# 17 pairs of column blocks as 2x2 block products in seven multiplications, in a hybrid trunk layer

## The chip, the cores and the metric

The kernel runs on one core of one Trainium2 chip. The metric is device time in microseconds (us) of one execution. The engines are named as the profile names them: PE is TensorE (matmuls; PEld its weight loads), DVE is VectorE, ACT is ScalarE, POOL is GpSimd, SP is SyncE, which here issues DMAs.

## The reference, cut to what matters

One layer over 512 prompt tokens and 64 sample tokens (T = 576), D = 1024, all fp32:

```python
h = _rmsnorm(x, norm_pre_w)
proj = h @ w_in                       # 1024 x 13344
glu_v, glu_g, conv_gate, z, xbc, dt_raw, q, xa_gate, gates = split(proj)

u = glu_v * sigmoid(glu_g)            # A: conv branch
c = causal_dwconv(u, width 31)
c = silu(layernorm(c)) * silu(conv_gate)
out_a = c @ conv_out_w
...                                   # B: state-space branch from z, xbc, dt_raw
out_b = y @ ssd_out_w
p = softmax(q @ mem_k / 16)           # C: 4 heads, 256 memory tokens
out_c = ((p @ mem_v) * silu(xa_gate)) @ xa_out_w

g = sigmoid(gates + gate_b)           # three gates, 1024 wide each
m = g[0] * out_a + g[1] * out_b + g[2] * out_c
x_new = x + _rmsnorm(m @ w_out, norm_post_w)
```

For the prompt, mem_k and mem_v are themselves a product, rmsnorm(mem) @ xa_kv_w; for the sample they come from a cache. The names used below for columns of w_in: `glu j` is the pair of column blocks gg (glu_g) and gv (glu_v); `cg` is conv_gate; `xg` is xa_gate; `g0`, `g1`, `g2` are the three gates. A block is 128 columns, so xg, g0, g1 and g2 have eight blocks each and q eight, two for each head.

## The kernel before, in words

The normed input is kept transposed, channels on partitions, as two tiles `hT[0]` and `hT[1]`: the rounded fp32r value and the remainder ("hi" and "lo"). Each weight block is 1024 x 128 and is one job of the list `order`. `prep_to` loads a job into `raw` by a DMA on SP's queue (512 KB), copies it to `whi` on ACT (L183) and lets DVE subtract to get `wlo` (L184); `W(name)` prepares up to LA = 2 jobs past the one asked for. Each of raw, whi and wlo has three buffers. `mac` (L204) multiplies in three passes (wh·rh, wh·rl, wl·rh), for eight k-tiles and two halves of 288 tokens: 48 matmuls of 288 columns for a block of w_in. `proj` returns the two PSUM banks of it.

The order of instructions on each engine is made by a scheduler at build time that estimates times; some are held in program order. The stages on PE, by the trace: the start and the state-space groups with glu 0 to 2 and out_b (to 503 us), glu 3 and 4 with the eight g1 blocks (to 573.7), four attention heads with their two xg blocks each and glu 5 to 7 (to 808), the g2 blocks in turn with the merge products oc (to 908), cg and g0 (to 1010), the merges oa (to 1062), and w_out.

Beside these, DVE works off a list of convolution steps in the background: for each of eight channel blocks 30 taps over 606 columns (L769, `c<-u,dww,c`), pushed in pairs by `push_conv` so that two blocks alternate, and taken n at a time by `bgrun(n)`.

A head of the attention computes k and q blocks, v, the scores (L886 to L888), a softmax (maxima L871 on DVE, exps L875 and scalings L880 on ACT), then xg's two blocks, then transposes P (L937, L944), splits it (L940, L941, L946), multiplies with v ("PV", again L886 to L888, and L956) and writes `oc` times the gate (L953, L959). The memory tokens' transposes (`memT`, L321 and L322) stand between the g1 blocks.

The core of the block product before the change:

```python
for i, (wh, wl, rh, rl) in enumerate(pairs, k0):
    for w, r, a in ((wh, rh, 0), (wh, rl, 1), (wl, rh, 2)):
        for o, (s, w_) in outs:
            m = nc.tensor.matmul(o, lhsT=w, rhs=r[:, s:s + w_], ...)
```

Of the kernel before, what the change touches and what calls it, by code (L numbers as in the profile page):

```python
# [15 lines left out]
T = 576  # L16
# [12 lines left out]
def hybrid_trunk_kernel(  # L29
# [134 lines left out]
    nprep = [0]  # L164

    def prep_to(n):
        while nprep[0] <= min(n, len(order) - 1):
# [14 lines left out]
            else:  # L182
                a = nc.scalar.activation(hi[:, :n_], raw[:, :n_], AF.Copy)  # L183
                b = nc.vector.tensor_tensor(lo[:, :n_], raw[:, :n_], hi[:, :n_].bitcast(F32), ALU.subtract)  # L184
# [534 lines left out]
    def glu(j, pool, tag, bufs, rate=4):  # L719
# [4 lines left out]
        bgrun(rate)  # L724
        pv = proj(f"gv{j}", HB)
        u = sx.tile([128, 640], F32, tag="xs", name="u", bufs=7)
        nc.gpsimd.memset(u[:, 0:30], 0.0)
        nc.gpsimd.tensor_copy(u[:, 542:572], sta.rearrange("p (r j) -> p r j", r=30)[:, :, j])
        nc.vector.scalar_tensor_tensor(v2(u[:, 30:542]), v2(t[:, 0:512]), 1.0, pv[:, :, 0:256], ALU.add, ALU.mult)
        nc.vector.scalar_tensor_tensor(u[:, 572:636], t[:, 512:T], 1.0, pv[:, 1, 256:320], ALU.add, ALU.mult)  # L730
        nc.gpsimd.tensor_scalar(utail[:, j, 0:30], u[:, 512:542], 0.5, None, ALU.mult)
        nc.gpsimd.tensor_scalar(utail[:, j, 30:60], u[:, 606:636], 0.5, None, ALU.mult)
        upad[j] = u
        bgrun(rate)
# [74 lines left out]

    for j in range(8):  # L810
        t = gate_t(f"g1_{j}", 1, j, sx, "xs", 7)
        nc.vector.scalar_tensor_tensor(ob[:, j], t, 1.0, ob[:, j], ALU.add, ALU.mult)
        nc.sync.dma_start(out=msc[j], in_=ob[:, j])
        bgrun(6)
        tr_act(mt_, j, memT, V_MEM, NMEM)
    stob.close()
    ocp = stx.enter_context(tc.tile_pool(name="ocp", bufs=1, side="right", reuse_waits="tile"))
# [72 lines left out]
    for h in range(4):  # L890
# [38 lines left out]
        for i in range(2):  # L929
            sgs.append(silu2(proj(f"xg{2 * h + i}"), sx, "xs", 7))  # L930
# [53 lines left out]
    ochl = [split(oc[:, j]) for j in range(8)]  # L984
    ocact = ([a for a, _ in ochl], [b for _, b in ochl])
# [39 lines left out]
    for j in range(8):  # L1025
        merge(j, 2, f"g2_{j}", f"oc{j}", ocact)
# [7 lines left out]
    stx.close()  # L1034
    stx = ExitStack()


    hlB = stx.enter_context(tc.tile_pool(name="hlB", bufs=8, side="right", reuse_waits="tile"))
    hl[0] = hlB
    chl, g0t = [], []  # L1040
    for j in range(8):
# [11 lines left out]
        g0t.append(gate_t(f"g0_{j}", 0, j, hlA, "lo", 8))  # L1053
# [138 lines left out]
```

## Time and profile before

| what | value |
|---|---|
| median of 3 runs | 1122.61 us (1122.55 to 1123.11) |
| the profiled execution | 1122.15 us, its span 1120.4 us, granted PE clock 0.999 |
| PE busy, instructions | 1109.5 us, 8285 |
| DVE busy, instructions | 829.1 us, 1268 |
| ACT busy, instructions | 481.9 us, 844 |
| POOL busy, instructions | 56.8 us, 146 |
| data moved | 120.74 MB, mean 108 GB/s |

The span runs from the first to the last instruction; the execution adds 1.75 us around it. An engine's busy time is a sum over the whole span, so its share says little about one stage: the windows show the stages apart. In a row of a group, `out<-in` gives the names of the tiles, then shapes, the count, the busy time and the mean of one in ns, and behind the bar the idle time of the engine just before these instructions with what ended it.

### The profile page before, as it was taken

The page shows a single profiled execution, that of the slowest core. Times are in us where ns is not written, and L with a number is a line of the kernel's source. Part 1 is how long each engine was busy: PE and PEld are TensorE (multiplying, and loading weights), DVE is VectorE, ACT ScalarE, POOL GpSimd, SP SyncE. Part 2 cuts the span into 40 slices and gives each one's busy share as a digit, 9 for nine tenths or more (in the row PEclk, how much of TensorE's full clock was granted, in tenths as well). Part 3 has the DMA queues.
Part 4 walks back from the last instruction along what each step waited for, and adds up shares of the span by engine and source line. Part 5 has one row for each costly group of instructions (what it writes and reads, how often), then busy time and mean ns, then how long its engine had stood idle before and what let it go on. Part 6 is the DMA issues. An engine that isn't in the chain of part 4 may idle for free.

```text
span 1120.4 us, 20083 instructions
## 1 busy us (share of the span) xinstructions
PE 1109.5 (99%) x8285; PEld 1070.9 (96%) x8285; DVE 829.1 (74%) x1268; ACT 481.9 (43%) x844; POOL 56.8 (5%) x146
## 2 busy tenths in 40 slices
PE   8999999999999999999999999999999999999997
PEld 8999999999999999999999999999999999999974
DVE  5778897578868885756899996998588868714533
ACT  5564664456436442543224453434421245522331
POOL 0100110011002100100000000000000000000000
PEclk9999999999999999999999999999999999999999
DMA  7354423442353232242445343434353234233502
GB/s 208 95 162 122 143 82 94 129 117 81 97 144 107 83 81 78 75 124 76 135 139 142 85 131 95 123 85 116 84 160 93 76 84 106 76 94 104 178 20 85
DMA packets 183233, 120.74 MB, mean 108 GB/s; under 512 B 12422, under 2 KB 173230, under 8 KB 183142
## 3 DMA queue, kind: packets, MB, share of 16 engines
q1 hardware_dynamic: 183142, 119.46, 37.4%
q8 instruction: 65, 1.06, 0.4%
q14 instruction: 26, 0.21, 0.1%
HBM read 110.13 MB, written 9.31 MB: 107 GB/s over the span
## 4 chain that ended last, share of the span: by engine, by line
PE 97%; DMA 1%; ACT 1%; SPq 0%; DVE 0%; issue 0%; DVEq 0%; ACTq 0%
PE mm L204 78%; PE ps L204 4%; PE ps L887 2%; PE ps L886 2%; PE ps L888 2%; PE ps L561 2%; PE ps L587 2%; PE ps L565 1%; DMA ob<-in_x_prompt_dram 1%; PE ps L526 1%; PE ps L1130 1%; PE ps L518 1%; PE mm L346 0%; DMA out_dram<-ho 0%; PE ps L483 0%; PE ps L937 0%
## 5 line engine op out<-in xcount | busy, mean ns | idle before, releaser
L204 PE MATMUL mm<-hT,whi 128*128 128x288 f32 (+2 forms) x3328 | 588.3, 297 | 0.8 <-DVE hT L280 0.3
L204 PEld LDWEIGHTS mm<-hT,whi 128*128 128x128 f32 x3328 | 495.1, 189 | 3.6 <-issue 1.3
L204 PE MATMUL mm<-hT,wlo 128*128 128x288 f32 (+2 forms) x1664 | 363.9, 297 | 0.0
L183 ACT ACTIVATE whi<-raw 128x1024 fp32r<-128x1024 f32 x152 | 160.9, 1059 | 401.0 <-PE mm L204 323.9
L204 PEld LDWEIGHTS mm<-hT,wlo 128*128 128x128 f32 x1664 | 273.6, 189 | 1.1 <-issue 0.7
L184 DVE TENSOR_TENSOR wlo<-raw,whi 128x1024 fp32r<-128x1024 f32 x152 | 185.8, 1222 | 116.0 <-ACT whi L183 115.7
L769 DVE SCALAR_TENSOR_TENSOR c<-u,dww,c 128x606 f32<-128x606 f32 x240 | 191.5, 844 | 0.0
L204 PE MATMUL mm<-hi,whi 128*128 128x288 f32 x512 | 111.4, 298 | 0.0
L204 PE MATMUL mm<-lo,whi 128*128 128x288 f32 x512 | 110.9, 296 | 0.0
L204 PE MATMUL mm<-hi,wlo 128*128 128x288 f32 x512 | 110.4, 296 | 0.0
L204 PEld LDWEIGHTS mm<-hi,whi 128*128 128x128 f32 x512 | 82.2, 189 | 0.9 <-issue 0.9
L204 PEld LDWEIGHTS mm<-hi,wlo 128*128 128x128 f32 x512 | 82.5, 188 | 0.2 <-issue 0.2
L204 PEld LDWEIGHTS mm<-lo,whi 128*128 128x128 f32 x512 | 82.5, 188 | 0.0
L454 DVE SCALAR_TENSOR_TENSOR acc<-xp,scw,acc 128x579 f32<-128x579 f32 x72 | 58.4, 815 | 3.1 <-ACT acc L450 1.9
L658 DVE TENSOR_TENSOR ob<-ob,mm 128x576 f32<-128x576 f32 x24 | 18.0, 750 | 16.3 <-PE mm L204 16.2
L547 ACT ACTIVATE M<-R,tok 128x128 f32<-128x128 f32 (+1 forms) x80 | 24.8, 379 | 12.3 <-PE ps L587 12.3
L446 POOL COPY tails<-xp 128x3 f32<-128x3 f32 x24 | 18.0, 751 | 193.2 <-ACT xp L444 187.9
L887 PE MATMUL ps<-lo,hi 128*128 128x512 f32 x64 | 25.3, 397 | 0.0
L888 PE MATMUL ps<-hi,lo 128*128 128x512 f32 x64 | 25.1, 395 | 0.0
L886 PE MATMUL ps<-hi 128*128 128x512 f32 x64 | 24.9, 397 | 0.0
L565 PEld LDWEIGHTS ps<-bc,h 128*128 128x128 f32 x128 | 16.5, 191 | 8.8 <-issue 6.6
L204 PE MATMUL ps<-whi,memT 128*128 128x256 f32 x128 | 23.5, 282 | 0.0
(292 smaller groups left out, 1287.8 us busy)
## 6 DMA issues: line engine op xcount, KB each, us to landing
raw<-in_w_in_dram SPq DMA_DIRECT2D x104, 512.0 KB
R<-scr SPq DMA_DIRECT2D x16, 512.0 KB
raw<-in_ssd_out_w_dram SPq DMA_DIRECT2D x16, 512.0 KB
raw<-in_xa_kv_w_dram SPq DMA_DIRECT2D x16, 512.0 KB
raw<-in_xa_out_w_dram SPq DMA_DIRECT2D x8, 512.0 KB
raw<-in_conv_out_w_dram SPq DMA_DIRECT2D x8, 512.0 KB
wraw<-in_w_out_dram SPq DMA_DIRECT2D x8, 512.0 KB
E<-scr SPq DMA_DIRECT2D x24, 128.0 KB
```

The costliest lines, as they stand in the source:

```text
L183: a = nc.scalar.activation(hi[:, :n_], raw[:, :n_], AF.Copy)
L184: b = nc.vector.tensor_tensor(lo[:, :n_], raw[:, :n_], hi[:, :n_].bitcast(F32), ALU.subtract)
L204: m = nc.tensor.matmul(o, lhsT=w, rhs=r[:, s:s + w_], start=(i == 0 and a == 0), stop=(i == n - 1 and a == 2),)
L454: nc.vector.scalar_tensor_tensor(acc, xp[:, r:r + 579], w4[:, r, jt:jt + 1], acc, ALU.mult, ALU.add)
L547: nc.scalar.activation(M[:, 4 + e, :], R[:nl, 4 + e, :], AF.Relu, scale=-1.0, bias=tok[:nl, 0, c, a + 4:a + 5])
L561: nc.tensor.matmul(pS, lhsT=bt[:nl], rhs=xw[:nl], start=True, stop=True)
L565: nc.tensor.matmul(po[:, nl * j:nl * j + nl], lhsT=h[:, 128 * j:128 * j + 128], rhs=gC[g][:, cs], start=True, stop=True,)
L587: nc.tensor.matmul(pd[o:o + 64, nl * (e // 2):nl * (e // 2) + nl], lhsT=xd[:nl, 64 * e:64 * e + 64], rhs=M[:, e, :], start=True, stop=True,)
L769: nc.vector.scalar_tensor_tensor(c, upad[j][:, r:r + NC], w31[:, r, j:j + 1], c, ALU.mult, ALU.add)
L886: nc.tensor.matmul(out, lhsT=wh, rhs=rh, start=(i == 0), stop=False)
L887: nc.tensor.matmul(out, lhsT=wh, rhs=rl, start=False, stop=False)
L888: nc.tensor.matmul(out, lhsT=wl, rhs=rh, start=False, stop=(i == n - 1))
```

## The change

All in `hybrid_trunk_kernel`:

- 17 pairs of blocks, in the order glu 3, g1 (four pairs), glu 4 to 7, xg (four), g2 (four), are computed in one stretch right behind out_b(3). For a pair the two blocks' columns, the two halves of the 1024 channels, and the two halves of the tokens make a 2x2 block product, which is done by seven products P1 to P7 (Strassen in Winograd's form) of 4 k-tiles x 3 passes = 12 matmuls of 288 columns.
- The combinations of hT (T1 to T4, hi and lo) are built once at the stretch's start by DVE and ACT. The weight-side sums (s1 to s4) are made by DVE for each pair, with their hi by ACT and lo by DVE. The blocks used unchanged (W11, W12, W22) get their hi by an ACT copy, and their lo by an ACT copy with factor -1 and a POOL-issued DMA that adds raw to it.
- The results are put together from three kinds of PSUM banks (X, Y, Z, two of each) with copies on ACT and adds on DVE. xg (with its silu) and g2 (its tanh) go to DRAM (`spill`) and are loaded back in the heads and merges.
- The 56 weight jobs behind the stretch get their lo by the same ACT copy and accumulating DMA in place of DVE's subtract.
- q0 and q1 come ahead of k0; memT's transposes stand behind q0 and q1 and no longer between g1 blocks. Convolution blocks from the third on are pushed singly; one background step is taken at every second slot of the stretch; the convolution's result is copied back over its input. The heads lose their xg and glu products. Some pools move.

```diff
-    for j in range(3, 5):
-        glu_jobs(j)
-    for j in range(8):
-        wjob(f"g1_{j}", w_in, C_G + 1024 + 128 * j)
+    hold = len(order)
     for h in range(4):
+        if h == 0:
+            for i in range(2):
+                wjob(f"q{i}", w_in, C_Q + 128 * i)
...
-                b = nc.vector.tensor_tensor(lo[:, :n_], raw[:, :n_], hi[:, :n_].bitcast(F32), ALU.subtract)
+                if nprep[0] < hold:
+                    b = nc.vector.tensor_tensor(lo[:, :n_], raw[:, :n_], hi[:, :n_].bitcast(F32), ALU.subtract)
+                else:
+                    nc.scalar.activation(lo[:, :n_], raw[:, :n_], AF.Copy, scale=-1.0)
+                    nc.gpsimd.dma_start(out=lo[:, :n_], in_=raw[:, :n_], accum_op=ALU.add)
...
+    for kp in range(2):
+        ks = slice(2 * kp, 2 * kp + 2)
+        a, b = blk(0, 1), blk(0, 0)
+        nc.vector.tensor_tensor(b, b, a, ALU.subtract)
+        put("T1", b)
+        c = blk(1, 1)
+        nc.vector.tensor_tensor(a, c, a, ALU.subtract)
+        put("T3", a)
+        nc.vector.scalar_tensor_tensor(c, b, -1.0, c, ALU.mult, ALU.subtract)
+        put("T2", c)
+        d = blk(1, 0)
+        nc.vector.scalar_tensor_tensor(d, c, -1.0, d, ALU.mult, ALU.subtract)
+        put("T4", d)
+    rhs = {"P1": hb(0, 0), "P2": hb(1, 0), "P3": hb(1, 1), "P4": comb["T4"], "P5": comb["T1"], "P6": comb["T2"], "P7": comb["T3"]}
...
+    def pair_pure(p, w, pr):
+        src = pw[p][w]
+        hi = sp.tile([128, 512], F32R, tag="ph", name="ph", bufs=5)
+        lo = sp.tile([128, 512], F32R, tag="pl", name="pl", bufs=4)
+        nc.scalar.activation(hi, src, AF.Copy)
+        nc.scalar.activation(lo, src, AF.Copy, scale=-1.0)
+        nc.gpsimd.dma_start(out=lo, in_=src, accum_op=ALU.add)
+        pw[p][pr] = hi, lo
+
+    def pair_sum(p, prs, sums):
+        sm = sp.tile([128, 1024], F32, tag="sm", name="sm", bufs=2)
+        for q, (nm, a, b) in enumerate(sums):
+            pw[p][nm] = sm[:, 512 * q:512 * q + 512]
+            nc.vector.tensor_tensor(pw[p][nm], pw[p][a], pw[p][b], ALU.add)
+        hi = wp.tile([128, 1024], F32R, tag="whi", name="whi", bufs=3)
+        lo = wp.tile([128, 1024], F32R, tag="wlo", name="wlo", bufs=3)
+        nc.scalar.activation(hi, sm, AF.Copy)
+        nc.vector.tensor_tensor(lo, sm, hi.bitcast(F32), ALU.subtract)
...
+    def product(p, pr, tag, start):
+        wh, wl = (w.rearrange("p (k c) -> p k c", k=4) for w in pw[p][pr])
+        rh, rl = rhs[pr]
+        o = bank(p, tag)
+        for k in range(4):
+            for w, r, a in ((wh, rh, 0), (wh, rl, 1), (wl, rh, 2)):
+                nc.tensor.matmul(
+                    o, lhsT=w[:, k], rhs=r[:, k], start=(start and k == 0 and a == 0), stop=(k == 3 and a == 2),
...
+    seq = [(0, "P2"), (0, "P1")]
+    for p in range(np_):
+        for pr, d in (("P5", 0), ("P6", 0), ("P2", 1), ("P7", 0), ("P1", 1), ("P3", 0), ("P4", 0)):
+            if p + d < np_:
+                seq.append((p + d, pr))
+    at = {e: i for i, e in enumerate(seq)}
...
+            (f - 14, lambda p=p: pair_load(p)),
+            (f - 6, lambda p=p: pair_pure(p, "W12", "P2")),
+            (at[p, "P1"] - 6, lambda p=p: pair_pure(p, "W11", "P1")),
+            (at[p, "P5"] - 5, lambda p=p: pair_sum(p, ("P5", "P6"), (("s1", "W21", "W22"), ("s2", "s1", "W11")))),
+            (at[p, "P7"] - 5, lambda p=p: pair_sum(p, ("P7", "P3"), (("s3", "W11", "W21"), ("s4", "s2", "W12")))),
+            (at[p, "P4"] - 6, lambda p=p: pair_pure(p, "W22", "P4")),
...
+    for i, (p, pr) in enumerate(seq):
+        while todo and todo[0][0] <= i:
+            todo.pop(0)[1]()
+        slot(p, pr)
+        if i % 2:
+            bgrun(1)
...
+    q0 = [proj(f"q{i}") for i in range(2)]
+    for j in range(8):
+        tr_act(mt_, j, memT, V_MEM, NMEM)
...
         for i in range(2):
-            sgs.append(silu2(proj(f"xg{2 * h + i}"), sx, "xs", 7))
+            sg = sx.tile([128, 640], F32, tag="bc", name="bc", bufs=4)[:, 0:T]
+            nc.sync.dma_start(out=sg, in_=spill["xg"][2 * h + i])
+            sgs.append(sg)
             bgrun(10)
...
-        if h > 0:
-            glu(4 + h, sx, "xs", 7)
-            if h != 2:
-                push_conv(3 + h, 4 + h)
...
-        t = gname if not isinstance(gname, str) else gate_t(gname, br, j, sx, "xs", 7)
+        if gname is None:
+            t = sx.tile([128, 640], F32, tag="bc", name="bc", bufs=4)[:, 0:T]
+            nc.sync.dma_start(out=t, in_=spill["g2"][j])
```

Three places of the order. First DVE at the end of out_b(3), before the change: the adds into ob (L658) stand apart, with weight splits, memT and the first taps between them.

```order
L658 TENSOR_TENSOR ob<-ob,mm 128x576 x2
L184 TENSOR_TENSOR wlo<-raw,whi 128x1024
L322 SCALAR_TENSOR_TENSOR memT_5822<-ps,vecs,memT_5821 128x256 x3
L658 TENSOR_TENSOR ob<-ob,mm 128x576 x2
L184 TENSOR_TENSOR wlo<-raw,whi 128x1024
L322 SCALAR_TENSOR_TENSOR memT_5822<-ps,vecs,memT_5821 128x256
L658 TENSOR_TENSOR ob<-ob,mm 128x576 x2
L184 TENSOR_TENSOR wlo<-raw,whi 128x1024
```

The same place on DVE after the change: the adds are L665; L817 rebuilds fp32 from hT's hi and lo, L826 to L834 combine token blocks, L823 takes the low part of a combination, L871 are weight sums.

```order
L665 TENSOR_TENSOR ob<-ob,mm 128x576 x6
L817 TENSOR_TENSOR ct<-hT_92,hT_93 128x576 x4
L826 TENSOR_TENSOR ct<-ct 128x576
L871 TENSOR_TENSOR sm<-raw,rawb 128x512
L871 TENSOR_TENSOR sm<-raw 128x512
L829 TENSOR_TENSOR ct<-ct 128x576
L871 TENSOR_TENSOR sm<-sm,raw 128x512
L831 SCALAR_TENSOR_TENSOR ct<-ct 128x576
L871 TENSOR_TENSOR sm<-sm,rawb 128x512
L823 TENSOR_TENSOR T1l<-ct,T1h 128x576
```

Behind the last add there now stands a run of combinations and sums, of which T1's first low half is the tenth; its second half comes 16 instructions later. On PE the products that need none of T1 to T4 stand ahead of the first that does (Z is P2's bank, Y that of P5):

```order
L892 MATMUL Z<-hT_92,ph 128x288
L892 MATMUL Z<-hT_93,ph 128x288
L892 MATMUL Z<-hT_92,pl 128x288
L892 MATMUL Y<-T1h,whi 128x288 x2
L892 MATMUL Y<-T1l,whi 128x288 x2
L892 MATMUL Y<-T1h,wlo 128x288
```

Second, ACT in the attention's head 0, before: exps, xg's gate (L463), scalings, one weight copy, and the splits of P (L940, L946).

```order
L875 ACTIVATE P,mx<-ps,mx 64x256
L463 ACTIVATE xs<-mm 128x576
L880 ACTIVATE P<-P,mx 128x256 x4
L880 ACTIVATE P<-P,mx 64x256
L183 ACTIVATE whi<-raw 128x1024
L463 ACTIVATE xs<-mm 128x576
L940 ACTIVATE pth<-ps 128x512 x2
L946 ACTIVATE pts<-ps 128x128
```

The same place after, where the two copies of a later weight and the split of the next head's q (L1116) stand ahead of the splits of P (L1155, L1161):

```order
L1088 ACTIVATE P,mx<-ps,mx 64x256
L1093 ACTIVATE P<-P,mx 128x256 x4
L1093 ACTIVATE P<-P,mx 64x256
L186 ACTIVATE whi<-raw 128x1024
L190 ACTIVATE wlo<-raw 128x1024
L1116 ACTIVATE qhi<-mm 128x576
L1155 ACTIVATE pth<-ps 128x512 x2
L1161 ACTIVATE pts<-ps 128x128
```

Both xg gates are gone from there, and a second weight copy has come.

Third, DVE behind the scores of head 3, before: P's low parts (L941), the four products into oc, and the eight low parts of oc's split, without a tap between them.

```order
L941 TENSOR_TENSOR ptl<-ps,pth 128x512 x2
L959 SCALAR_TENSOR_TENSOR oc<-ps,xs 128x64
L953 SCALAR_TENSOR_TENSOR oc<-ps,xs 128x512 x2
L959 SCALAR_TENSOR_TENSOR oc<-ps,xs 128x64
L606 TENSOR_TENSOR lo<-oc,hi 128x576 x8
```

After, the same steps are L1156, L1174, L1168 and L613, and background taps (L773) stand between them:

```order
L1156 TENSOR_TENSOR ptl<-ps,pth 128x512
L1174 SCALAR_TENSOR_TENSOR oc<-ps,bc 128x64
L773 SCALAR_TENSOR_TENSOR c<-u,dww,c 128x606 x4
L1168 SCALAR_TENSOR_TENSOR oc<-ps,bc 128x512
L773 SCALAR_TENSOR_TENSOR c<-u,dww,c 128x606
L1168 SCALAR_TENSOR_TENSOR oc<-ps,bc 128x512
L1174 SCALAR_TENSOR_TENSOR oc<-ps,bc 128x64
L773 SCALAR_TENSOR_TENSOR c<-u,dww,c 128x606
L613 TENSOR_TENSOR lo<-oc,hi 128x576 x2
```

On PE no product stands between the scores of head 3 and its transposes of P any more.

More of the change, by code (lines that the diff above doesn't have):

```diff
@@ L164, in hybrid_trunk_kernel @@
     nprep = [0]
+    limit = [hold - 1]
     def prep_to(n):
-        while nprep[0] <= min(n, len(order) - 1):
+        while nprep[0] <= min(n, len(order) - 1, limit[0]):
             name, src, c0, r0, kk, cols = order[nprep[0]]
@@ L723, in glu, with gate @@
         nc.scalar.activation(t[:, 512:T], pg[:, 1, 256:320], AF.Tanh, scale=0.5)
-        bgrun(rate)
         pv = proj(f"gv{j}", HB)
[L726 to L734, printed above, removed]
+        def gate(a, b):
+            nc.vector.scalar_tensor_tensor(v2(a), v2(t[:, 0:512]), 1.0, pv[:, :, 0:256], ALU.add, ALU.mult)
+            nc.vector.scalar_tensor_tensor(b, t[:, 512:T], 1.0, pv[:, 1, 256:320], ALU.add, ALU.mult)
+        u_tile(j, t, gate)
     for j in range(3):
@@ new lines, in hybrid_trunk_kernel, with bank @@
+    pb = [{} for _ in pairs]
+    def bank(p, tag):
+        if tag not in pb[p]:
+            pb[p][tag] = px.tile([128, 512], F32, tag=tag, name=tag, bufs=2)[:, 0:288]
+        return pb[p][tag]
+    def product(p, pr, tag, start):
[6 more added lines that the diff above has]
+                    o, lhsT=w[:, k], rhs=r[:, k], start=(start and k == 0 and a == 0), stop=(k == 3 and a == 2),
+                    skip_group_check=True,
+                )
@@ new lines, in pair_c1, with pair_c2, gate @@
+    def pair_c1(p):
+        kind, i = pairs[p]
+        c = pb[p]["c1"]
+        if kind == "glu":
+            nc.scalar.activation(c, c, AF.Tanh, scale=0.5)
+        else:
+            pair_use(kind, 2 * i, c)
+    def pair_c2(p):
+        kind, i = pairs[p]
+        c = pb[p]["c2"]
+        if kind == "glu":
+            t = pb[p]["c1"]
+            def gate(a, b):
+                nc.vector.scalar_tensor_tensor(a, t[:, 0:512], 1.0, c[:, 0:512], ALU.add, ALU.mult)
+                nc.vector.scalar_tensor_tensor(b, t[:, 512:T], 1.0, c[:, 512:T], ALU.add, ALU.mult)
+            u_tile(i, t, gate)
+            push_conv(i)
+        else:
+            pair_use(kind, 2 * i + 1, c)
@@ new lines, in hybrid_trunk_kernel @@
+    np_ = len(pairs)
+    seq = [(0, "P2"), (0, "P1")]
[4 more added lines that the diff above has]
+    at = {e: i for i, e in enumerate(seq)}
+    todo = []
+    for p in range(np_):
+        f = at[p, "P2"]
+        todo += [
+            (f - 14, lambda p=p: pair_load(p)),
[4 more added lines that the diff above has]
+            (at[p, "P4"] - 6, lambda p=p: pair_pure(p, "W22", "P4")),
+        ]
@@ L808, in hybrid_trunk_kernel @@
             )
[L810 to L815, printed above, removed]
     stob.close()
-    ocp = stx.enter_context(tc.tile_pool(name="ocp", bufs=1, side="right", reuse_waits="tile"))
+    sto = ExitStack()
+    ocp = sto.enter_context(tc.tile_pool(name="ocp", bufs=1, side="right", reuse_waits="tile"))
     oc = ocp.tile([128, 8, T], F32, name="oc")
```

174 lines of the change are left out of this document (139 added, 35 removed).

## The prediction

> **What bounds the kernel now.** I read the profile in this order: busy time by engine, the chain that ended last, the windows by stage, the costliest groups, then the waits of ACT and DVE in one head of the attention. First, busy time and the chain:
>
> ```profile
> PE 1109.5 (99%) x8285; PEld 1070.9 (96%) x8285; DVE 829.1 (74%) x1268; ACT 481.9 (43%) x844; POOL 56.8 (5%) x146
> PE 97%; DMA 1%; ACT 1%; SPq 0%; DVE 0%; issue 0%; DVEq 0%; ACTq 0%
> q1 hardware_dynamic: 183142, 119.46, 37.4%
> ```
>
> PE is the bound: 1109.5 of 1120.4 us, and 97% of the chain. DMA has room at 37.4%, and q1 is the one data queue: no POOL-issued DMA occurs. So a matmul removed counts in full, and each PE wait that the change makes counts in full against it. What the new waits cost depends on how much room DVE and ACT have beside PE, stage by stage (columns: window, its length, then busy time and instructions of PE, PEld, DVE, ACT, POOL; granted clock, DMA share, GB/s):
>
> ```profile
> 503.00:573.70 70.70, 70.70 (x533) 70.70 (x532) 55.95 (x72) 20.53 (x27) 2.71 (x6) 1.00 0.38 108
> 573.70:808.00 234.30, 234.30 (x1797) 231.31 (x1796) 199.67 (x291) 97.71 (x183) 6.13 (x12) 1.00 0.40 110
> 808.00:908.00 100.00, 100.00 (x753) 100.00 (x752) 76.02 (x94) 23.55 (x28) 0.00 (x0) 1.00 0.38 109
> ```
>
> These stages are glu3, glu4 and g1; the four heads with xg and glu5 to 7; the g2 and oc merges. PE has no gap in any of them, at full clock, and in the heads DVE is already busy 199.67 of 234.30 us. The change empties the heads of PE work and leaves DVE's there.
>
> **Removed.** 17 pairs were 34 blocks of 48 matmuls, 1632; they become 17 x 7 products x 12 = 1428. The price of one comes from the chain's longest piece, the two rows behind it from the groups:
>
> ```profile
> 503.05 70.40 PE mm L204 x528
> L204 PE MATMUL mm<-hT,whi 128*128 128x288 f32 (+2 forms) x3328 | 588.3, 297 | 0.8 <-DVE hT L280 0.3
> L204 PEld LDWEIGHTS mm<-hT,whi 128*128 128x128 f32 x3328 | 495.1, 189 | 3.6 <-issue 1.3
> ```
>
> 70.40/528 = 0.1333 us per matmul (the 297 ns of a single one overlaps its neighbours). There is one weight load per matmul already, 3328 of each, so smaller products lose no reuse. 204 x 0.1333 = **-27.2 us**, for certain as long as PE is fed.
>
> **The stretch's start.** The order shows that DVE must first finish the eight adds of out_b(3), the last of which needs PE's last matmul of that stage. Only then do T1 to T4 and the first weight sums start, and the second half of T1's low part (which P5 of pair 0 needs) is the 28th DVE instruction behind that add: 19 of 576 elements, 7 of 512, 2 of 1024. Durations are taken start to start, since neighbours overlap a little:
>
> ```profile
> 870.85 1.22 DVE L184 TENSOR_TENSOR wlo<-raw,whi 128x1024 fp32r<-128x1024 f32 x1
> 871.99 0.75 DVE L992 TENSOR_TENSOR ob<-ob,xs 128x576 f32<-128x576 f32 x1
> 872.66 1.61 DVE L769 SCALAR_TENSOR_TENSOR c<-u,dww,c 128x606 f32<-128x606 f32 x2
> 876.88 4.65 DVE L769 SCALAR_TENSOR_TENSOR c<-u,dww,c 128x606 f32<-128x606 f32 x6
> 609.31 0.68 DVE L827 TENSOR_TENSOR vvl<-kk,vvh 128x512 fp32r<-128x512 f32 x1
> 609.90 0.85 DVE L769 SCALAR_TENSOR_TENSOR c<-u,dww,c 128x606 f32<-128x606 f32 x1
> ```
>
> 1024 elements: 871.99 - 870.85 = 1.14; 576: 0.67; 512: 609.90 - 609.31 = 0.59; a tap: 4.65/6 = 0.78. So 19 x 0.67 + 7 x 0.59 + 2 x 1.14 = 19.1, with the last add's 0.75 some 19.9 us behind PE's last matmul. PE meanwhile has P2 of pairs 0 to 2, P1 of pairs 0 and 1, and the first half of P5(0): 66 matmuls, 8.8 us. It waits 11.1. Then P6 and P7 of pair 0 catch up with T2's second half, with P5's bank copy, and with a whi buffer that ACT can refill only when P6 has read it: 0.4 + 0.5 + 1.5. **+13.5 us**, bounds 8 (if combinations and sums hardly wait for ACT and fewer stand ahead) and 18.
>
> **The steady stretch.** Per pair PE needs 84 x 0.1333 = 11.2 us. DVE: four sums of 512, two low parts of 1024, three bank reads of 288 (about 0.4), glu or gate products (1.3 on average), 3.5 taps: 2.4 + 2.3 + 1.2 + 1.3 + 2.7 = 9.9. ACT's copies come to about 7.8 (of 512 at 0.53 and of 1024 at 0.97, from the starts below). Both fit: **0**. At mean durations instead of spacings
>
> ```profile
> L184 DVE TENSOR_TENSOR wlo<-raw,whi 128x1024 fp32r<-128x1024 f32 x152 | 185.8, 1222 | 116.0 <-ACT whi L183 115.7
> L769 DVE SCALAR_TENSOR_TENSOR c<-u,dww,c 128x606 f32<-128x606 f32 x240 | 191.5, 844 | 0.0
> ```
>
> DVE needs 10.9 of 11.2, so the upper bound is half a microsecond a pair, +8. The xg and g2 spills (32 transfers of 288 KB, write and read) ride on a queue at 37%: 0.
>
> At its end no further pair fills P6 -> ACT copy -> P7 -> DVE read -> P4 of pair 16: **+1.4**.
>
> **memT.** Its 8 transposes leave the g1 stage, where PE had other work, and stand between q0, q1 and k0, whose product reads memT:
>
> ```profile
> L183 ACT ACTIVATE whi<-raw 128x1024 fp32r<-128x1024 f32 x152 | 160.9, 1059 | 401.0 <-PE mm L204 323.9
> L321 ACT ACTIVATE memT<-ps,vecs 128x256 fp32r<-128x256 f32 x8 | 3.4, 463 | 0.0
> L322 DVE SCALAR_TENSOR_TENSOR memT<-ps,vecs,memT 128x256 fp32r<-128x256 f32 x8 | 3.6, 478 | 0.0
> ```
>
> ACT's weight copies wait mostly for PE to release a buffer (323.9 of 401.0 us idle): here whi and the new second copy of v0 stand ahead of the memT copies and wait for q1's end, 1.94, then come eight pairs of 0.46 and 0.48, pipelined with k0's k-tiles. **+2.9**, bounds 1 and 5.
>
> **Heads 0 to 2.** Before, the softmax ran under 96 matmuls of xg and 27 more:
>
> ```profile
> 608.73 12.80 PE mm L204 x96
> 621.52 0.87 PE ps L937 x8
> 622.40 0.27 PE ps L944 x2
> 622.66 3.79 PE mm L204 x27
> ```
>
> P's transposes (L937) came 12.8 us after the scores and their splits had 3.8 us more. Now one block of the next head's q stands there (48 matmuls, 6.4 us), and four matmuls of the next (0.5) before PV. ACT, as head 0 ran:
>
> ```profile
> 612.61 0.48 ACT L875 ACTIVATE P<-ps,mx 128x256 f32<-128x256 f32 x1 [5.33 <-DVE mx L872]
> 617.74 2.11 ACT L880 ACTIVATE P<-P,mx 128x256 f32<-128x256 f32 x5
> 621.29 1.06 ACT L183 ACTIVATE whi<-raw 128x1024 fp32r<-128x1024 f32 x1 [1.45 <-PE mm L204]
> 622.26 0.63 ACT L463 ACTIVATE xs<-mm 128x576 f32<-128x576 f32 x1
> 622.79 1.07 ACT L940 ACTIVATE pth<-ps 128x512 fp32r<-128x512 f32 x2
> ```
>
> Three maxima and five exps and scalings take about 5.8 us behind the last score, which the 6.4 covers. But in ACT's new order whi and wlo of a later weight (0.97 each, whi only once q's product releases the buffer) and q's split (0.53) stand ahead of the splits of P: 6.4 + 1.94 + 0.53 + 0.5 puts the first split of P at about 9.4 and the last at 10.3, where PE asks at 6.4 + 1.1 + 0.5 = 8.0 (1.1 is the two transposing rows). 1.4 in front of the prompt's PV and 0.7 at the sample's: 2.1 a head, **+6.3**, bounds 0 (if scheduling slack hides it) and 12.
>
> **Head 3.** Before, 101 matmuls followed its scores:
>
> ```profile
> 773.15 13.45 PE mm L204 x101
> ```
>
> Now its P transposes follow directly: first P at 4.6 us, PE otherwise empty, 1.1 more lost between splits and PV, which ends at about 9.9. Then the oc merge needs all of oc split; its first low part stands behind P's last split (8.9), four products into oc and six taps on DVE: 8.9 + 2 x 0.3 + 2 x 0.75 + 6 x 0.78 = 15.7 (the four products estimated from the rows of 576), while PE runs dry at 11.3 after the utail transposes. 4.6 + 1.1 + 4.4: **+10.1**, bounds 6 and 13.
>
> **Accumulating DMAs.** The 56 weights behind the stretch lose DVE's 1.14 us of split and get an ACT copy and a POOL-issued DMA of up to 512 KB that adds raw into it; pure blocks the same with 256 KB. No row shows one; the nearest are
>
> ```profile
> 214.66 4.07 DMA out_dram<-ho
> 3.98 8.66 DMA ob<-in_x_prompt_dram
> ```
>
> Taking 4.07 (256 KB, alone): whi, wlo and the DMA need 6.0 us of the two blocks' lead, 12.8, and the pure blocks have six products' lead, 9.6. Only q of the next head, whose buffer comes free at the last moment, sees 0.2: inside the 2.1. At 8.66 (a load amid others) blocks still fit, 10.6 in 12.8, but the heads lose 4.6 each. The Trainium skill, DMA: Bandwidth & Descriptors, section "Anatomy of one DMA — SWDGE (gpsimd) path", gives 2.0 us plus bytes/436e3 per us; by it 512 KB would take an estimated 3.2 us and the sum would stay. No run here shows that yet.
>
> The LN chain behind the merges costs 0: DVE's work behind cg6 is some 70 instructions at about 0.7, 50 us, and PE's cg7 and g0 are 9 x 48 x 0.1333 = 57.6.
>
> Sum: -27.2 + 13.5 + 0 + 1.4 + 2.9 + 6.3 + 10.1 = **+7.0**. The profiled execution took 1122.15 us (span 1120.4), 0.46 below the median of the runs, so 1122.61 + 7.0 = 1129.6: **1130 us**.
>
> **Rivals.** A, faster: the attention's waits vanish. For it speaks that head 3 had a spare 13.45 us of cover in before and PE never waited; against it that this cover is just what leaves. Without the 16.4 us of the heads the sum is -9.4: 1113 us. It decides once the heads lose under 7.2 together; a shorter start (8) would give 1108.
>
> B, no change: heads 0 to 2 are hidden, head 3 is not: 7.0 - 6.3 = +0.7, 1123.3. For it: each of those waits is at most 2.1, and ACT is busy only 97.71 of 234.30 us in the heads, so one place in its order decides.
>
> C, much slower: the accumulating DMAs land late, 8.66 for 4.07: 4.6 x 3 heads = +14, 1144 us, and if pure blocks in the stretch miss their 9.6 too, more. For it: POOL's queue carries nothing like them now, and 107 pieces (56 weights, 51 pure blocks) would hang on it. Against: DMA is 37% busy. The Trainium skill, SBUF — State Buffer, section "SBUF: two separate sides", says that a DMA issued by GpSimd cannot get its descriptors written while VectorE runs an operation in a two-port mode. By that rule the late case would come about wherever DVE runs such operations; the rows above show none that runs faster per element than the others (576 at 0.67 us and 1024 at 1.14 us are both 1.1 to 1.2 ns), and no run here shows a POOL-issued DMA beside them.
>
> That seven products don't give what they promise (PE slower per matmul) I hold for excluded by the load count above.
>
> **Chances.** The forecast 0.43, with its own range 1125 to 1139 (its bounds: start 8 to 18, stretch up to +8); A 0.24; B 0.14; C 0.19. A measurement can tell this kernel from no change at about 0.2%, 1120.4 to 1124.9: faster is A, 0.24, same is B, 0.14, slower the rest, 0.62. The range leaves out A's shorter start and C's worst end: 1111 to 1148.
>
> **What would show it.** Right: a PE gap near 11 us with DVE busy through it right behind out_b(3); in the stretch no PE gap over 0.5 us and DVE at 85 to 95%; PE waiting on ACT's splits of P in each head and about 10 us in head 3. Wrong: DVE above 97% in the stretch with PE stopping each pair; PE or ACT released by POOL's DMA in the rows; heads without a gap.

## The result, and the profile after

The changed kernel takes 1178.96 us (median of 4 runs, 1174.68 to 1180.58), the kernel before 1122.86 on the same chip (1122.55 to 1123.59): ratio 1.0493, 95% interval 1.0465 to 1.0521, 5% slower. The prediction said 1130, with a range of its own from 1125 to 1139 and 1148 as the worst end: the direction was right, the size was not. The profiled execution has a span of 1178.5 us, 58.1 more than before. First its page: busy time, chain, the granted PE clock in 40 slices, the data queues, and the median time from issue to landing of the accumulating DMAs.

```profile
PE 1113.5 (94%) x8081; PEld 1061.3 (90%) x8081; DVE 854.8 (73%) x1355; ACT 620.0 (53%) x1081; POOL 157.6 (13%) x253
PE 78%; DMA 9%; issue 7%; ACT 2%; DVE 2%; POOL 0%; SPq 0%; DVEq 0%; POOLq 0%; ACTq 0%
PEclk9999999999999999979999999789988999999999
q1 hardware_dynamic: 188294, 128.90, 37.6%
q0 software_dynamic: 15408, 42.74, 20.3%
wlo<-raw POOLq DMA_DIRECT2D x56, 512.0 KB, 5.6
pl<-rawb POOLq DMA_DIRECT2D x34, 256.0 KB, 4.5
```

PE has 204 instructions less and yet 4 us more of busy time. The clock row says why. Before, it was 9 throughout:

```profile
PEclk9999999999999999999999999999999999999999
```

Now it has slices of 7 and 8, and matmuls there took longer. DMA, 1% of the chain before, is 9%. The windows by stage (columns as in the prediction), from the end of out_b(3) to the start of the oc merge:

```profile
501.00:533.00 32.00, 21.33 (x112) 18.37 (x111) 26.82 (x39) 17.90 (x31) 7.98 (x9) 0.79 0.70 140
533.00:714.00 181.00, 174.51 (x1300) 172.41 (x1298) 148.19 (x219) 117.49 (x208) 49.97 (x53) 1.00 0.77 183
714.00:744.00 30.00, 21.30 (x138) 19.10 (x138) 6.51 (x15) 17.05 (x28) 3.47 (x4) 0.86 0.80 207
744.00:780.00 36.00, 29.17 (x204) 27.39 (x204) 22.24 (x38) 24.30 (x46) 4.31 (x5) 0.93 0.78 181
780.00:820.00 40.00, 35.13 (x240) 33.49 (x238) 30.64 (x48) 19.45 (x36) 4.31 (x5) 0.87 0.79 193
820.00:865.00 45.00, 39.73 (x269) 37.46 (x268) 34.66 (x53) 23.82 (x43) 5.19 (x6) 0.89 0.74 178
865.00:920.00 55.00, 44.73 (x291) 40.14 (x290) 45.63 (x72) 29.34 (x55) 5.19 (x6) 0.88 0.69 163
```

These are the stretch's start, its steady part, its end with memT, and the heads. Where PE has gaps the clock is 0.79 to 0.93; in the steady part it is 1.00 and 1300 instructions take 174.51, 0.134 each, as before. From 920 us to the end PE has no more gaps than before. What PE waited for (in total, times, longest):

```profile
PE ps L211 <- DMA wlo<-raw: 8.0, 4, 3.5
PE Z L892 <- DMA pl<-rawb: 7.4, 5, 2.8
PE mm L211 <- DMA wlo<-raw: 7.1, 4, 3.0
PE ps L326 <- DVE mt L269: 6.4, 2, 6.2
PE ps L1152 <- ACT P L1093: 5.5, 1, 5.5
PE ps L1099 <- ACT pth L1155: 3.0, 3, 1.0
PE X L892 <- ACT u L953: 2.6, 2, 1.3
PE Y L892 <- ACT T1h L822: 2.3, 1, 2.3
```

22.5 of these microseconds are accumulating DMAs: 15.1 for weights of the heads (`wlo`), 7.4 for pure blocks (`pl`). What a gap does to the clock is read from PE's timeline. The first three rows are P2 right behind a gap of 2.79 us at the stretch's start, the last three the same product 19 us later:

```profile
517.55 0.61 PE L892 MATMUL Z<-hT,pl 128*128 128x288 f32 x1 [2.79 <-DMA pl<-rawb]
517.96 0.68 PE L892 MATMUL Z<-hT,ph 128*128 128x288 f32 x2
518.44 0.44 PE L892 MATMUL Z<-hT,pl 128*128 128x288 f32 x1
518.68 0.68 PE L892 MATMUL Z<-hT,ph 128*128 128x288 f32 x2
...
536.50 0.43 PE L892 MATMUL Z<-hT,ph 128*128 128x288 f32 x2
536.76 0.29 PE L892 MATMUL Z<-hT,pl 128*128 128x288 f32 x1
536.90 0.42 PE L892 MATMUL Z<-hT,ph 128*128 128x288 f32 x2
```

Three matmuls start to start: 518.68 - 517.96 = 0.72 us, 0.24 each, against 536.90 - 536.50 = 0.40, 0.133 each. In the trace's clock record the clock is half for 13.65 us from 516.98 on, and again in eight pieces of 3.4 to 10.2 us up to 909.5. PE worked 47.3 us in these pieces; half of that, an estimated 23.6 us, is a cost on top of the waits.

### The profile page after: what moved, and what is told of

Same layout as the page of the kernel before. It is cut to its first block, busy times and chain, and to the rows that moved or that the text cites. A ratio compares the mean times of both kernels' runs of the same rounds, so it can differ in the third digit from the quotient of the medians.

```text
span 1178.5 us, 20510 instructions
## 1 busy us (share of the span) xinstructions
PE 1113.5 (94%) x8081; PEld 1061.3 (90%) x8081; DVE 854.8 (73%) x1355; ACT 620.0 (53%) x1081; POOL 157.6 (13%) x253
## 4 chain that ended last, share of the span: by engine, by line
PE 78%; DMA 9%; issue 7%; ACT 2%; DVE 2%; POOL 0%; SPq 0%; DVEq 0%; POOLq 0%; ACTq 0%
PE mm L211 51%; PE X L892 7%; DMA wlo<-raw 4%; PE Y L892 4%; DMA pl<-rawb 2%; PE Z L892 2%; PE ps L211 2%; PE ps L1100 2%; PE ps L568 2%; PE ps L594 2%; PE ps L1101 1%; PE ps L1099 1%; PE ps L572 1%; DVE c L773 1%; DMA rawb<-in_w_in_dram 1%
## 5 line engine op out<-in xcount | busy, mean ns | idle before, releaser
L211 PE MATMUL mm<-hT,whi 128*128 128x288 f32 (+2 forms) x2240 | 401.4, 299 | 0.8 <-DVE hT L287 0.3
L211 PEld LDWEIGHTS mm<-hT,whi 128*128 128x128 f32 x2240 | 338.4, 191 | 3.5 <-issue 1.3
L211 PE MATMUL mm<-hT,wlo 128*128 128x288 f32 (+2 forms) x1120 | 249.3, 301 | 7.1 <-DMA wlo<-raw 7.1
L186 ACT ACTIVATE whi<-raw 128x1024 fp32r<-128x1024 f32 x118 | 124.8, 1058 | 246.0 <-PE mm L211 161.7
L773 DVE SCALAR_TENSOR_TENSOR c<-u,dww,c 128x606 f32<-128x606 f32 x240 | 202.2, 845 | 4.5 <-ACT c L766 0.8
L211 PEld LDWEIGHTS mm<-hT,wlo 128*128 128x128 f32 x1120 | 187.3, 191 | 10.1 <-DMA wlo<-raw 8.9
L188 DVE TENSOR_TENSOR wlo<-raw,whi 128x1024 fp32r<-128x1024 f32 x62 | 75.7, 1221 | 37.2 <-ACT whi L186 36.8
L191 POOL DMA_DIRECT2D wlo<-raw x56 | 48.7, 869 | 354.9 <-ACT wlo L190 238.3
L190 ACT ACTIVATE wlo<-raw 128x1024 fp32r<-128x1024 f32 x56 | 58.7, 1049 | 14.0 <-PE ps L211 9.4
L875 DVE TENSOR_TENSOR wlo<-sm,whi 128x1024 fp32r<-128x1024 f32 x34 | 41.5, 1220 | 10.1 <-ACT whi L874 10.0
L453 POOL COPY tails<-xp 128x3 f32<-128x3 f32 x24 | 18.9, 787 | 192.5 <-ACT xp L451 188.0
L874 ACT ACTIVATE whi<-sm 128x1024 fp32r<-128x1024 f32 x34 | 35.9, 1055 | 15.3 <-PE X L892 14.5
L864 POOL DMA_DIRECT2D pl<-rawb x34 | 30.2, 895 | 99.3 <-ACT pl L863 98.9
L665 DVE TENSOR_TENSOR ob<-ob,mm 128x576 f32<-128x576 f32 x24 | 18.0, 749 | 22.0 <-PE mm L211 21.9
```

What stands on the lines that cost most here:

```text
L190: nc.scalar.activation(lo[:, :n_], raw[:, :n_], AF.Copy, scale=-1.0)
L191: nc.gpsimd.dma_start(out=lo[:, :n_], in_=raw[:, :n_], accum_op=ALU.add)
L211: m = nc.tensor.matmul(o, lhsT=w, rhs=r[:, s:s + w_], start=(i == 0 and a == 0), stop=(i == n - 1 and a == 2),)
L773: nc.vector.scalar_tensor_tensor(c, upad[j][:, r:r + NC], w31[:, r, j:j + 1], c, ALU.mult, ALU.add)
L864: nc.gpsimd.dma_start(out=lo, in_=src, accum_op=ALU.add)
L874: nc.scalar.activation(hi, sm, AF.Copy)
```

## The experiments

The theory after the first look: the loss is accumulating DMAs that land late, and every PE wait is paid again in half clock. The rival: DVE is the limit from the stretch to the LayerNorm, and whatever is taken from one place comes back in another.

**e1.** lo of the 56 weights behind the stretch by DVE.

```diff
-                if nprep[0] < hold:
-                    b = nc.vector.tensor_tensor(lo..., raw..., hi..., ALU.subtract)
-                else:
-                    nc.scalar.activation(lo[:, :n_], raw[:, :n_], AF.Copy, scale=-1.0)
-                    nc.gpsimd.dma_start(out=lo[:, :n_], in_=raw[:, :n_], accum_op=ALU.add)
+                eng = nc.vector if nprep[0] < hold else nc.vector
+                b = eng.tensor_tensor(lo..., raw..., hi..., ALU.subtract)
```

> The 56 weights behind the stretch get their lo by DVE's subtract again, as before the change; the stretch keeps its accumulating DMAs. Theory (PE waits for late accumulating DMAs, and each such wait also halves the granted clock for some us): the 15.1 us in which PE waits for DMA wlo<-raw go, and with them part of the 34 us that PE works at half clock behind the stretch (worth half of it), so 15 to 25 us less; DVE gets 56 x 1.14 = 64 us more beside PE, of which 10 to 15 may come back as waits in head 3 and at the LayerNorm: 1160 to 1172. Rival (DVE paces what follows the stretch, the DMAs were its relief): the DMA waits turn into DVE waits of the same size or more: 1177 to 1200.

1176.13 us, ratio 1.0476 (1.0457 to 1.0494): 3 less, between the two ranges. From the stretch's end to the first oc product it takes 159 us instead of 195, so the waits for DMA are gone and 36 us with them. But two waits of PE appear that were not there, at the split of the convolution's result and at the LayerNorm's sums:

```profile
PE mm L208 <- ACT hi L608: 14.5, 1, 14.5
PE ps L1217 <- ACT sh L1213: 9.6, 1, 9.6
881.00:930.00 49.00, 49.00 (x368) 49.00 (x369) 45.37 (x59) 9.88 (x11) 0.00 (x0) 1.00 0.48 147
```

Up to there DVE was busy 45.37 of 49.00 us: its taps came late. Both theories hold in part: the path by a second ACT copy and an accumulating DMA, with the half clock behind its waits, cost this part of the program about 36 us, and in this order DVE cannot take the work for nothing.

**e2.** The pure blocks' lo by DVE (`nc.vector.tensor_tensor(lo, src, hi.bitcast(F32), ALU.subtract)` for L863 and L864).

> The pure blocks of the stretch get their lo by DVE's subtract (51 of 128x512), the weights behind the stretch keep their accumulating DMAs. Theory: 7.4 us of PE waits for DMA pl<-rawb go and 2 to 4 us of half clock at the start; DVE's work per pair rises from about 9.9 to 11.7 us against PE's 11.2, which gives back up to 8: 1170 to 1180. Rival (DVE paces the stretch already): every subtract shows, 51 x 0.59 = 30 us less what the waits were: 1195 or more.

1176.60 us, ratio 1.0478 (1.0463 to 1.0494). The waits for `pl` by DMA went, the wait for T1 grew from 2.3 to 6.8 us, since DVE has more to do ahead of it; the stretch is 1 us shorter. In the stretch DMA and DVE are worth the same. That is the theory's range, and the rival (DVE paces the stretch, 1195 or more) is out: in the steady part, 534 to 715 us, DVE was busy 171.75 of 181.00 us, and the 51 subtracts did not lengthen it.

**e3.** Both kinds of lo by a subtract on POOL, without the second ACT copy and the DMA.

> Both kinds of lo are made by a subtract on POOL, no second ACT copy, no accumulating DMA. If the landing of 4.5 to 5.6 us is what PE waits for and POOL takes under about 2.5 us for 128x1024, the 22.5 us of waits go with 10 to 15 us of half clock: 1140 to 1150. If POOL is slow (5 us or more for 128x1024) it is as late as the DMA: 1175 or more.

1216.39 us, ratio 1.0833 (1.0804 to 1.0862), 37 more. That lies in the range for a slow POOL (1175 or more), but POOL was not as slow as that forecast's condition, 5 us. POOL's subtract itself and the taps on DVE:

```profile
L188 POOL TENSOR_TENSOR wlo<-raw,whi 128x1024 fp32r<-128x1024 f32 x56 | 154.2, 2758 | 269.6 <-ACT whi L186 267.9 <-ACT mean L1222 1.6
L770 DVE SCALAR_TENSOR_TENSOR c<-u,dww,c 128x606 f32<-128x606 f32 x240 | 269.9, 1128 | 3.5
```

POOL's 2.76 us are about half of the 5.6 that the DMA took. But the same 240 taps took 1128 ns each instead of 845, though nothing in them changed: DVE and POOL hinder each other. The Trainium skill, SBUF — State Buffer, section "SBUF: two separate sides", says that the two share a pair of ports as an exclusive lock, taken by a DVE operation with two inputs in SBUF against a POOL operation that reads SBUF. Taps of just this kind, 283 ns longer, agree with that.

**e4 and e11.** Useless matmuls in PE's waits, to keep the clock up: 40 ahead of memT and 36 in head 3 (e4), 36 in head 3 alone (e11).

```diff
+        if h == 3:
+            dummies(36)      # matmul(p[:, 0:128], lhsT=ident, rhs=ident)
```

> Useless matmuls (ident by ident, 128 columns) are put on PE where it stands idle: 40 ahead of memT's transposes (wait 6.2 us), 36 between head 3's scores and P's transposes (wait 5.5 us). Nothing else changes. Theory (the clock is halved after idle PE and that is a cost of its own): both half-clock stretches of 10.24 us there vanish, PE was busy about 6.5 us in each, half of which is saved: 5 to 7 us less, 1172 to 1174. Rival (the slow matmuls there are latency behind the wait, or the clock has another cause): no change within 1 us, or up to 3 us more where the useless work is longer than the wait.

> The changed kernel with 36 useless matmuls only in head 3's wait (5.5 us) between scores and P's transposes. Theory (half clock as a cost of its own): the 10.24 us of half clock behind it vanish, and from the first transposition of P to the first oc product with lo it takes about 8.4 us instead of 11.8, 3 to 4 less; the whole 1175 to 1176. Rival: 11.8 there as before and no gain.

e4 1177.02 us, ratio 1.0479 (1.0462 to 1.0497); e11 1178.65, ratio 1.048 (1.045 to 1.051), no gain that can be told. In place, the clock came back. First the transposes of P in head 3 of the changed kernel, then the filling and the same transposes in e11:

```profile
902.71 1.97 PE L1152 MATMUL ps<-ident,P 128*128 128x128 f32 x8 [5.53 <-ACT P L1093]
```

```profile
899.74 6.75 PE L1017 MATMUL ps<-ident 128*128 128x128 f32 x59
906.33 1.04 PE L1159 MATMUL ps<-ident,P 128*128 128x128 f32 x8
```

Eight transposes take 1.04 us instead of 1.97, and from there to the first oc product with lo it is 8.5 us instead of 11.8 (7.9 in e4). But each useless matmul is two records of 0.114 us: 36 take 8.2 us (59 of the 72 records are in this row), more than the wait of 5.5, and P's transposes come 3.6 us later. So the price of the half clock in this place is shown (3.3, where 3 to 4 were expected), and a gain in the whole is not: my filling was too long.

**e5.** As e1, with a background tap at three of four slots (`if i % 4 != 3` for `if i % 2`).

> As e1_jobs_dve (lo of the weights behind the stretch by DVE), and the stretch takes a background tap at three of four slots instead of every second one (30 taps more, 23 us of DVE). In e1 PE waited 24 us for the LayerNorm because DVE's taps were late, while DVE was busy 180 of 220 us in the stretch. Theory (DVE's work from the stretch to the LayerNorm is a second bound, the DMAs only moved it): the 24 us shrink to under 5, the stretch grows by at most 5: 1152 to 1160. Rival (the LayerNorm's wait has another cause, or the stretch is DVE's limit already): 1172 or more.

1162.11 us, ratio 1.0347 (1.0332 to 1.0362), 14 less than e1. The waits at the LayerNorm are gone (from the first oc product to the end of the oa merges 206 us instead of 238). But the stretch took 17.6 us more for 23 us of taps, over three times what I had expected, and now waits for the pure blocks:

```profile
PE Z L889 <- DMA pl<-rawb: 13.7, 11, 3.2
```

The whole is 2 us above the theory's range and 10 below the rival's. What is shown is that the LayerNorm's waits go when the taps come earlier. Why these taps cost the stretch 17.6 us is not: DVE was busy only 164.56 of 196.00 us in its steady part, and the pure blocks, for which PE waited, landed sooner than in the changed kernel (median 3.7 us against 4.6), so they were issued late. It is not the amount of DVE's work alone, since e2 put 51 subtracts of 0.59 us, 30 us, into the same stretch without lengthening it (and took as many ACT copies and DMAs out). The place of the work in each engine's order counts, and the chain behind it stays open.

**e6.** glu 3 directly (96 matmuls) as cover for T1 to T4.

```diff
+    glu_jobs(3)
     hold = len(order)
...
+    glu(3, sp, "ct", 4)        # behind T1 to T4 in the program, beside them on PE
...
+    pairs = [("g1", m) for m in range(4)] + ...
...
+    push_conv(3)
```

> glu 3 is computed directly (96 matmuls) between out_b(3) and the block products of 16 pairs, beside which DVE builds T1 to T4. All else as in the changed kernel. Theory (the start's loss is PE waiting for DVE's combinations plus 13.65 us of half clock behind it): 12 us of waits and 4.5 of clock go, 12 matmuls more cost 1.6: 13 to 15 us less, 1164 to 1167. Rival (the start is paced by the first accumulating DMAs, 3.5 us of PE waits there): under 6 us less, 1173 or more.

1166.51 us, ratio 1.0389 (1.0372 to 1.0406), inside the expected 1164 to 1167, though 12.5 less is just under the 13 to 15. It would have been more but for a new wait, of PE for the bank that the tanh had not read yet; the tanh's buffer is one that the combinations use, and with a buffer of its own (e9) this wait is gone:

```profile
PE Z L894 <- ACT ct L743: 9.8, 1, 9.8
```

**e7.** The memory tokens' tiles over buffers that come free earlier (4200 columns of an unused tile ahead of them).

> The memory tokens' tiles lie over buffers that the stretch is done with earlier (rawb) and no longer over T4 and the spill's source tiles; nothing else changes. Theory (memT's transposes wait 6.2 us because the load can only start when the spilled g2 has left the buffer below it): 5 to 8 us less, with the half clock there: 1171 to 1174. Rival (the load is late for its place on SP's queue or DVE is): no change within 2 us.

1176.45 us, ratio 1.0469 (1.0448 to 1.0491), 2.5 less, near the rival's 2 and far from the theory's 5 to 8. SP's queue:

```profile
723.90 0.38 SPq L176 DMA_DIRECT2D raw<-in_xa_kv_w_dram  x1
724.38 0.64 SPq L933 DMA_DIRECT2D spill_g<-ct  x1
726.37 0.38 SPq L176 DMA_DIRECT2D raw<-in_xa_kv_w_dram  x1
726.86 1.90 SPq L1012 DMA_DIRECT2D mt<-in_mem_prompt_dram  x2
```

The load of mt is issued behind two weight loads, which wait for a free buffer, and the last spill; it starts 2.3 us earlier than in the changed kernel (729.20), no more.

**e8.** xg directly in the heads again, 13 pairs left.

> xg's eight blocks are computed directly in the heads again (13 pairs in the stretch): 48 matmuls more, 6.4 us. Theory (the heads lose because their cover left: softmax and splits 10, the accumulating DMAs of k and q 15, and 17 of half clock): at least two thirds of these 42 go: 1155 to 1162. Rival (DVE's taps and ACT's copies pace the heads, not the cover): the waits stay and 6.4 us come on top, 1180 to 1188.

1153.65 us, ratio 1.0276 (1.0258 to 1.0295), 25.3 less with 48 matmuls more, and better than the theory's 1155 to 1162. The waits for `wlo` fell from 15.1 to 5.4 us, those for P's split from 3.0 to 1.7, and head 3's 5.5 us are gone.

**e9 and e10.** e9: e8 and e6 together (the tanh in a buffer of its own), and mt loaded on POOL's queue over the early buffers. e10: besides, lo of k, q, v and xg by DVE (`if nprep[0] < hold or name[0] in "kqvx"`).

> Three repairs in one: xg directly in the heads (e8), glu 3 directly as cover for T1 to T4 (e6, with its tanh in a buffer of its own, since in e6 PE then waited 9.8 us for that buffer), and the memory tokens loaded on POOL's queue over buffers that are free early (in e7 the load stood on SP's queue behind a weight load that waited for its buffer). 12 pairs are left, 19.2 us of products saved. Theory (the losses are separate waits and their half clocks, so the repairs add up): 1153.7 - 12.5 - 10 to 14 - 6 to 11 = 1116 to 1125. Rival (DVE's work is what is conserved, and each repair only moves the wait): 1130 or more.

> As e9, and the 32 weights of the heads (k, q, v, xg) get their lo by DVE; oc, cg, g0, oa keep the accumulating DMA. Theory: the heads' 5.4 us of waits for wlo<-raw and their half clock go, the heads with xg have room for 32 x 1.14 = 36 us of DVE: 4 to 8 us less than e9. Rival (DVE is short up to the LayerNorm): as late as e9 or later, with a PE wait at the LayerNorm.

e9 1144.97 us, ratio 1.0195 (1.0181 to 1.0209): 20 to 29 short of the sum of the repairs, and so in the rival's range. In e9 PE still waited for accumulating DMAs in the heads:

```profile
PE mm L214 <- DMA wlo<-raw: 3.0, 3, 1.4
PE ps L214 <- DMA wlo<-raw: 2.5, 1, 2.5
```

e10 1126.07, ratio 1.0027 (1.0017 to 1.0037): 18.9 less, two to five times what I expected. So the accumulating DMAs in the heads cost far more than these 5.5 us of waits put down to them. It also speaks against the rival's reason (DVE's work is what is conserved): e10 gives DVE 32 subtracts more and gains. One reason for the size stands in ACT's rows of e9:

```profile
842.28 1.06 ACT L189 ACTIVATE whi<-raw 128x1024 fp32r<-128x1024 f32 x1 [7.41 <-DMA raw<-in_w_in_dram]
```

The hi copy waits for the load, not only lo for its sum: an accumulating DMA reads raw, so raw's buffer stays taken until it lands, and the next load is issued that much later. In e9's trace three of these DMAs land at 833.22, 836.11 and 839.94 us, and the next three loads into raw are issued at 833.28, 836.16 and 839.95. PE's wait is then put down to what it happens to meet last.

**e12.** As e10, with the two tail copies of each glu block on ACT in place of POOL. In e10 PE still stood for 4 us, and this is what POOL did before:

```profile
537.14 0.61 PE L899 MATMUL X<-T3h,whi 128*128 128x288 f32 x1 [3.98 <-ACT u L960]
```

```profile
518.23 8.48 POOL L737 TENSOR_SCALAR utail<-u 128x30 f32<-128x30 f32 x1 [9.99 <-DVE u L752]
526.68 0.28 POOL L738 TENSOR_SCALAR utail<-u 128x30 f32<-128x30 f32 x1
526.91 1.80 POOL L871 DMA_DIRECT2D pl<-rawb  x2
```

A copy of 30 columns took 8.48 us while DVE worked without a break (8.50 of the 8.50 us from 518.20 on), its twin 0.28, and the DMAs stood behind it.

> As e10, with the two small tail copies of each glu block on ACT in place of POOL. In e10 one of them (30 columns) occupied POOL for 8.48 us right behind DVE's run of combinations, three accumulating DMAs were issued behind it, the buffers they read came free late and PE waited 4.0 us for pair 3's load, with 6.83 us of half clock behind. Theory (POOL waits for the port that DVE uses, and an accumulating DMA keeps its source's buffer): that wait and its half clock go, 5 to 8 us less than e10's 1126.1: 1118 to 1121, faster than before by 0.2 to 0.4%. Rival (pair 3's load is late for the DMA queues alone): within 2 us of e10.

1121.95 us, ratio 0.9991 (0.9982 to 1.0001): 4.1 less than e10, where 5 to 8 were expected, and no difference to before that can be measured. PE's wait at P7 of the first pair is 0.7 instead of 4.0 and the half clock there is gone. Twelve pairs, 144 matmuls less (19.2 us), end where the kernel before was:

```profile
PE 1095.6 (98%) x8141; PEld 1052.6 (94%) x8141; DVE 858.7 (77%) x1344; ACT 578.3 (52%) x1024; POOL 108.2 (10%) x200
```

## Why the prediction was wrong

Each term is measured between two events on PE, less the work in between at the rates before:

| term | forecast | measured |
|---|---|---|
| 204 matmuls less | -27.2 | -27.2 |
| start of the stretch | +13.5 | +18.4 |
| steady stretch | 0 (0 to 8) | +6.9 |
| its end | +1.4 | +1.9 |
| memT | +2.9 (1 to 5) | +9.8 |
| heads 0 to 2 | +6.3 (0 to 12) | +36.6 |
| head 3 | +10.1 (6 to 13) | +11.5 |
| sum | +7.0 | +57.9 (span: +58.1) |

- **The removed matmuls** came out exactly: 0.134 us each in the steady stretch, and one weight load each.
- **The start** was right in its mechanism and near in its waits: P5 went on with T1's second half at 522.62 us, 21 us behind the last matmul of out_b(3) (forecast 19.9), and PE waited 12.0 us up to 534.8, in gaps of 0.4 to 2.8 and not in the one gap near 11 that I had named as a sign. Missing is the half clock, worth 4.5 (PE busy 8.9 us in 13.65). e6 bears the size out: the cover gave back 12.5.
- **The steady stretch** lies inside its bounds by luck. The bound of 8 was for DVE, and DVE was busy only 148.19 of 181.00 us, 82%, under the 85 to 95 that I had named as a sign. 3.9 of the 5.1 us that PE waited there were for pure blocks by DMA, whose lead I had held for enough.
- **memT** failed in a step that I left out. I moved the transposes and not what stands ahead of them: the load of the memory tokens and their normalization moved behind the stretch as well. Before, that load was issued at 474.1 us, and the transposes ran at 485.6 to 503.0 us among the matmuls of out_b(3) and at 573.3 and 579.9, not between the g1 blocks as I had it. The chain of the changed kernel shows the load on the path:

```profile
723.58 5.57 DMA spill_g<-ct
729.20 5.25 DMA mt<-in_mem_prompt_dram
734.47 1.15 ACT sqm L265 x2
735.64 1.28 ACT L266
```

- **Heads 0 to 2** is the term that decided. The step that failed reads "whi, wlo and the DMA need 6.0 us of the two blocks' lead, 12.8". The lead is 12.8 only between blocks of 48 matmuls; k and v have 24 (0.119 us each, 2.9), so their successors have 5.7 to 9.2. And the DMA took 5.6, not 4.07, on queues busy 0.7 to 0.8 in these windows. The splits of P behind q's, which I had priced at 2.1 a head, cost 1.0 (3.0 in three heads). So what I had named as a sign of being wrong, PE released by POOL's DMA, stands in the rows, and rival C was right that these DMAs land late. That its 14 us are near the 15.1 of waits measured is in part luck, since it took 8.66 us for a landing and not a shorter lead. What it lacked is that such waits come again as half clock, 13.4 us in these heads (26.8 us of work in it), and that the loads behind become late too. All waits of PE in the heads and this half clock make some 33.6 of the 36.6; the rest I can't put down to anything. Rival B, which had heads 0 to 2 hidden, falls with this term.
- **Head 3** came out within 1.4 us, its sum by luck: 5.5 of wait for P (forecast 4.6) bears the mechanism out, but lo's wait was 1.7 (4.4), and 3.4 of half clock, not in the forecast, made up for it.
- **The clock** is the omission common to all: I read 1.00 in every window before and priced each wait at its own length. The Trainium skill, TensorE: Matmul & The Clock Gate, section "HAM oscillation — how this bites in real kernels", warns of PE gaps over about 3.4 us. This case goes further: the clock fell at 516.98 us behind gaps of 0.4 to 2.8 us, none longer, and in heads 0 to 2 behind gaps of 0.8 to 3.5. When a gap has this effect stays open: one of 1.75 us at 692.83 left the clock full, and one of 1.00 at 777.26 was followed by half clock from 779.80 on.
- **The rule on descriptors** that rival C weighed by the Trainium skill (SBUF — State Buffer, section "SBUF: two separate sides": a POOL-issued DMA can't get its descriptors written while DVE runs an operation in a two-port mode) was not put to the test, since no row shows an operation of DVE in such a mode. With the operations that ran, DVE made no difference: an accumulating DMA issued at 727.82 us with DVE idle landed after 5.30 us, one at 764.64 with DVE busy three quarters of the time after 4.61; first packets came 1.43 us behind the issue in both. Late landings go with traffic instead: the slowest (a pure block, 8.5 us) had 2.2 MB of loads beside it. That is read from the trace and was not tried. POOL's own instructions are another matter (e3, e12).
- **Rival A** (the heads hide everything) had it that PE never waited in the heads before. e8 shows the opposite: the cover of xg was worth 25.3 us plus the 6.4 that it costs.

Open is the total price of the clock: 23.6 us by the records, shown in place by e4 and e11, but no run removed it without adding work. Not settled either is how the 18.9 us between e9 and e10 divide between late sums, late loads and half clock, and no run took the second ACT copy away without the DMA, so their shares are not told apart.

## What to carry to other kernels

When PE is at 99%, an algorithm that trades matmuls for vector work is worth its matmuls only as far as every other engine keeps its lead: here 1.6 us of PE per pair were paid with some 3.6 us of DVE (5.9 for sums, low parts and bank reads, less the two subtracts of 1.14), and DVE's subtracts of 1.14 went to a path of some 6.6 us (ACT copy 0.95, then 5.6 from POOL's issue to the landing). With xg's cover back, the runs that gave the heads' subtracts back to DVE were the faster ones (e10, e12), so there a busy DVE was the lesser cost. Price a removed cover by what it covered, in every chain that ran below it, and check the lead at the shortest job, not at the usual one. In these runs PE gaps, some of them of 1 us, were often followed by 3 to 17 us at half clock, so a forecast of waits needs a term for the clock.

## What the runs showed that I had not expected

- An accumulating DMA of 512 KB inside the chip's buffers took 4.5 to 8.0 us from the start of its issue, median 5.6, kept its source's buffer for that time, and cost POOL 0.87 us to issue.
- POOL and DVE slow each other: taps at 1128 ns instead of 845 (e3), a 30-column copy on POOL at 8.48 us instead of 0.28 (e10).
- Half clock often follows gaps of 1 to 3 us, in pieces that are multiples of 3.41 us: 3.41 to 17.07, and one of 27.31 in e1 around its waits of 9.6 and 14.5. The runs of such kernels also spread more: 1174.68 to 1180.58 here against 1122.55 to 1123.59 before.
